# First half of the tokens first between stages, chunks split ahead behind its transposes, and the norm's diagonal on ScalarE

## The chip, the cores and the metric

The kernel runs on one core of a Trainium2 chip. A core has a matrix engine (TensorE, PE in the profile; PEld is its weight load), VectorE (DVE), ScalarE (ACT), GpSimd (POOL) and an engine that issues loads (SP). Each takes its own instructions strictly in the order in which the program gives them. The metric is the device time of one execution in microseconds (us); less is better.

## The reference, cut to what matters

256 tokens of width 1024 go through two models. The first has two layers, each a mixer and a mixture of experts; the second has two layers (l0, l1) of attention and MLP, whose norms are scaled and shifted by a projection of a condition vector.

```python
def first_block(x, ...):
    h = x
    for i in range(DEPTH):                       # 2
        mix = gla_mixer(h, ...) if i % 2 == 0 else mlstm_mixer(h, ...)
        h = layer_norm(ALPHA * h + mix, ln_g[i, 0], ln_b[i, 0])
        ffn = grouped_moe(h, router_w, moe_w1[i], moe_w3[i], moe_w2[i])
        h = layer_norm(ALPHA * h + ffn, ln_g[i, 1], ln_b[i, 1])
    return h

def rms(x, g):
    return x * lax.rsqrt(jnp.mean(x * x, axis=-1, keepdims=True) + EPS) * g

def second_block(x, c, w_ada, b_ada, ...):
    for l in range(DEPTH):                       # 2
        ada = silu(c) @ w_ada[l] + b_ada[l]
        sh1, sc1, gt1, sh2, sc2, gt2 = jnp.split(ada, 6)
        h = rms(x, g_mix[l]) * (1.0 + sc1) + sh1
        parts = jnp.split(h @ w_in[l], IN_SPLITS)
        ...                                      # two attentions, gated sum
        x = x + gt1 * (mixed @ w_out[l])
        h2 = rms(x, g_mlp[l]) * (1.0 + sc2) + sh2
        x = x + gt2 * (jnp.square(jax.nn.relu(h2 @ w_ff1[l])) @ w_ff2[l])
```

## The kernel before, in words

**Stages.** The stages run one after another: gla, moe0, mlstm, moe1, then l0 and l1. The state `h` stays on chip as two halves of 128 tokens (128 partitions x 1024); the code calls a half `mt`. A dense product needs its input turned (width on the partitions) and in two parts that sum to it, `X_H` and `X_L`, and its weights likewise as `hi` and `lo`. Three products make one: hi with X_H, lo with X_H, hi with X_L.

**Weight chunks.** Weights arrive by SP's loads into a ring of buffers `w`, 512 x 512 each, and are split in halves called chunks. `S.split` makes a chunk: ScalarE (or VectorE, by a modelled clock) casts `hi<-w`, then VectorE subtracts, `lo<-w,hi`. A dense stage calls `S.ahead(1 + LOOK)` and `S.chunk()` for each chunk, LOOK being 2: asking for its first chunk, it issues the splits of the first three, unless they were made before, and with each later chunk one more. `S.early(n)` is `S.ahead(n)` with the subtraction on GpSimd in place of VectorE. There are four buffers for hi and four for lo.

**Between stages.** Five times a stage ends in a residual and a norm whose result the next stage multiplies: moe0 to mlstm, moe1 to l0, l0's out projection to its MLP, l0 to l1, and l1's out projection to its MLP. The residual is VectorE's `res<-mm,gt` (or `res<-acc,gt`) and `h<-h,res`, by blocks of 512 columns. `rms_T` then does one half `mt`: ScalarE's squares `aff_q,ss<-h` (issued with the residual), VectorE's `rs<-ss` and `rs<-rs`, GpSimd's power `rs<-rs,mhalf`, a diagonal matrix `diag<-ident,rs` of the 128 factors. `affine_T` goes on: 16 rows of TensorE multiply the half's eight blocks of 128 x 128 with that diagonal, which turns and scales them (`tpd<-diag,h`); ScalarE makes X_H in eight pieces, `X_H<-tpd,mod`; VectorE makes eight pieces `aff_t<-tpd,mod` and two subtractions `X_L<-aff_t,X_H`. `mod` holds the scale and shift of the norm. At moe0 to mlstm a layer norm is done instead, with plain transposes and no diagonal (`ln_mv`, `ln_rs`, `ln_nb`).

**Order around it.** `out_proj` (TensorE's matmuls of the attention's last projection) and the MLP's `down(last)` take the first half's matmuls, then the second half's; at the end of each half `emit` issues the residual and the squares and pushes `rms_T` as a generator onto a list. A generator goes on by one step with each `B.tick()`, which stands behind groups of matmuls; where it yields a number it stays away for so many ticks. So the number `wait` of `affine_T` says how many groups of matmuls TensorE gets ahead of the diagonal products; where the stage has none left, the next stage's first request for the half's X (`x.wait(mt)`) ticks on until it is there. At the end of a `moe` a string sets the order in which the two halves' tails take their steps, with 'e' for an early split. The next stage's first product (`dense`) multiplies its first four chunks with the first half of the tokens and then with the second half.

**The ada stream.** The condition's projections (`w_ada`) are computed beside the other work by a generator, `ada_cols`, in quarter steps: ScalarE `ada_t<-ada_w,ccol`, VectorE a multiply-add `ada_t<-ada_w,ccol,ada_t` and an addition; after each fourth a transpose and a reduction to `part`, and TensorE folds it (`bgp<-part,fold`) into the columns of `mod`. Layer l0 has 48 quarter steps. A quarter step is issued only when a modelled clock of the engines (`calm`) finds its engine free, and at most ten ticks later. `ada_need(l, 9)`, in the first half's `emit` of `out_proj`, issues what is missing of the first 40, on which the MLP's `mod` rests.

All operations are recorded through one helper, so that the profile gives nearly all of them line 175; tiles tell them apart.

Of the kernel before, what the change touches and what calls it, by code (L numbers as in the profile page):

```python
# [30 lines left out]
AF = mybir.ActivationFunctionType  # L31
OP = mybir.AluOpType
# [195 lines left out]
def tile_model(ctx: ExitStack, tc: tile.TileContext, I, out, stages=None, h_in=None):  # L228
# [421 lines left out]
    def out_proj(x, between, emit, busy=lambda: False, each=False):  # L650


        B.hold = True
        if busy():
            B.hold = False
        ps = [[mm_ps() for _ in range(2)] for _ in range(2)]
        for nb in range(2):
            dense(x, None, KT=4, ps=ps[nb], last=False)
        between()
        chs = []  # L660
        for mt in range(2):
            for c in range(4):
                if mt == 0:
                    S.ahead(min(1 + LOOK, 4 - c))
                    chs.append(S.chunk())
                nb, c2 = divmod(c, 2)
                for k in range(2):
                    group_mm(ps[nb][mt], x, 4 + 2 * c2 + k, mt, chs[c], k, False, c2 == 1 and k == 1)
                    if k or each:
                        B.tick()  # L670
                if hooks and busy():
                    hooks.pop(0)(bg_ps())
                if mt == 1 and c in (1, 2):
                    S.early(c)
                if c2 == 1:
                    emit(mt, nb, ps[nb][mt])
        B.hold = False
# [16 lines left out]
    def affine_T(x, src, mt, gcol_, bcol_, diag=None, wait=0):  # L694


        if wait:
            yield wait
        pss = []
        for q in range(2):  # L700
            blk = lambda k: src[:, (4 * q + k) * P:(4 * q + k + 1) * P]
            if diag is None:
                ps = transpose4(blk)
            else:
                ps = mm_ps((P, 4, P), name="tpd")
                for k in range(4):
                    PE.matmul(ps[:, k], blk(k), diag, start=True, stop=True)
            pss.append(ps)
        yield
        ts = []  # L710
        for q in range(2):

            t = aff.tile([P, 4, P], F32, name="aff_t", bufs=2)
            for k in range(4):
                ka, kt = 4 * q + k, 4 * (1 - q) + k
                V.tensor_scalar(t[:, k], pss[1 - q][:, k], gcol_[:, kt:kt + 1], bcol_[:, kt:kt + 1], op0=OP.mult, op1=OP.add)
                A.activation(x.dst(0, ka, ka + 1, mt)[:, 0], pss[q][:, k], AF.Identity, scale=gcol_[:, ka:ka + 1],
                             bias=bcol_[:, ka:ka + 1])
            ts.append(t)
        for q in range(2):  # L720
            hi, lo = x.dst(0, 4 * q, 4 * q + 4, mt), x.dst(1, 4 * q, 4 * q + 4, mt)
            V.tensor_tensor(lo, ts[1 - q], hi.bitcast(F32), op=OP.subtract)
        x.ready.add(mt)
# [416 lines left out]
    def moe(l, R, tail, order, prep):  # L1140
# [344 lines left out]
        S.spare = 0  # L1485
        combine(7, y)
        tails = [tail(mt, acc[mt]) for mt in range(2)]
        n = 0
        for i in order:
            if i == 'e':  # L1490
                n += 1
                S.early(n)
            else:
                next(tails[int(i)])
        for t in tails:
            B.push(t, True)

# [484 lines left out]
    def rms_T(x, l, which, mt, wait=0, ss=None):  # L1982


        if ss is None:
            ss = small.tile([P, 2], F32, name="ss")
            for nb in range(2):
                square(ss, mt, nb)
            yield
        rs = small.tile([P, 1], F32, name="rs")  # L1990
        V.tensor_tensor(rs, ss[:, 0:1], ss[:, 1:2], op=OP.add)
        rstd(rs, rs, 1e-6, 1.0 / D)
        yield
        diag = aff.tile([P, P], F32, name="diag", bufs=2)
        V.tensor_scalar(diag, c_ident, rs, None, op0=OP.mult)
        yield from affine_T(x, h[:, mt], mt, mod[:, l, which, 0], mod[:, l, which, 1], diag, wait)

    def rms_in(l, which):
# [17 lines left out]
    def attention(l, x, at):  # L2016
# [284 lines left out]
        def emit(mt, nb, ps):  # L2301
            n = slice(nb * 512, (nb + 1) * 512)
            t = at.tile([P, 512], F32, name="res", tag="xs", bufs=4)
            V.tensor_tensor(t, ps, gt[:, n], op=OP.mult)
            V.tensor_tensor(h[:, mt, n], h[:, mt, n], t, op=OP.add)
            if nb == 0:
                sss.append(small.tile([P, 2], F32, name="ss"))
            square(sss[mt], mt, nb)
            if nb:
                if mt == 0:  # L2310
                    ada_need(l, 9)
                B.push(rms_T(x2, l, 1, mt, 1 + 3 * mt, sss[mt]), True)
        sss = []
        out_proj(mT, B.drain_urgent, emit, lambda: (l, 9) not in ada_done)
        B.hold = True
# [2 lines left out]
    def mlp(l, x, mp):  # L2318
# [29 lines left out]
        def down(fb, f, last=False, emit=None):  # L2348
            chs = []
            if not last:  # L2350
                for kt in range(4):
                    S.ahead(1 + LOOK)
                    ch = S.chunk()
                    for mt in range(2):
                        for nb in range(2):
                            n = slice(nb * 512, (nb + 1) * 512)
                            mm3(acc[mt][nb], f.get(0, kt, mt), f.get(1, kt, mt), ch[0][:, n], ch[1][:, n],
                                fb == 0 and kt == 0, False)
                    B.tick()
                    B.tick()  # L2360
                return
            for mt in range(2):
                for kt in range(4):
                    if mt == 0:
                        S.ahead(min(1 + LOOK, 4 - kt))
                        chs.append(S.chunk())
                    ch = chs[kt]
                    for nb in range(2):
                        n = slice(nb * 512, (nb + 1) * 512)
                        mm3(acc[mt][nb], f.get(0, kt, mt), f.get(1, kt, mt), ch[0][:, n], ch[1][:, n],  # L2370
                            False, kt == 3)
                    B.tick()
                    if mt == 1 and kt in (1, 2) and S.chunk_at < len(S.chunks):
                        S.early(kt)
                emit(mt)

        fx = []
# [16 lines left out]
        def emit(mt):  # L2394
# [9 lines left out]
            if nxt is None:  # L2404
                store(mt)
            else:
                B.push(rms_T(nxt, 1, 0, mt, 1 + 3 * mt, sss[mt]), True)
        sss = []
        down(7, fx[-1], True, emit)
        return nxt  # L2410
# [165 lines left out]
    if first:  # L2576
        with tc.tile_pool(name="ring_b", bufs=RB) as rb, tc.tile_pool(name="rt", bufs=1) as rp, \
# [12 lines left out]
            for i, s in enumerate(first):  # L2590
                nxt = (first + second)[i + 1] if i + 1 < len(first + second) else None
                with tc.tile_pool(name="ph_" + s, bufs=1) as ph:
# [8 lines left out]
                    else:  # L2601
# [9 lines left out]
                        B.hold = True  # L2611
                        if nxt == "mlstm":
                            xin = mlstm_in()
                            moe(l, R, lambda mt, ps: mlstm_tail(xin, mt, ps), '0e1e01', lambda: None)
                        else:
                            xin = rms_in(0, 0) if nxt == "l0" else None
                            moe(l, R, lambda mt, ps: plain_tail(mt, ps, rows, xin),
                                '0e1e00000111' if nxt else '010101',
                                lambda: rows.extend(plain_rows(l, ph)))
                if nxt is None:  # L2620
                    for mt in range(2):
# [43 lines left out]
```

## Time and profile before

| what | value |
| --- | --- |
| median of 3 runs | 1690.78 us (1687.51 to 1692.52) |
| the profiled execution, whose trace is read below | 1689.23 us |
| its span in the trace, 22598 instructions | 1687.3 us |
| mean granted TensorE clock in it | 0.969 of full speed |
| TensorE busy | 1556.7 us (92%) |
| VectorE busy | 977.3 us (58%) |
| ScalarE busy | 687.9 us (41%) |
| GpSimd busy | 224.7 us (13%) |

The profiled execution's time is its span with 1.9 us around it. Busy shares are means over stages of quite different kinds; a stage with TensorE at its full rate and a window between stages read differently, so the trace is read by windows.

### The profile page before, as it was taken

Reading aid. Unit: us, or ns where it says so; the run is one execution under the profiler, and the core shown is the slowest. Engines: PE = TensorE matmul, PEld = TensorE weight load, DVE = VectorE, ACT = ScalarE, POOL = GpSimd, SP = SyncE. Lnnn points to the kernel's source line nnn. Section 1 sums busy time; section 2 is a strip of 40 time slices with the busy share of each in tenths; the row PEclk is TensorE's granted clock in tenths of the full one; section 3 lists DMA queues with packets and bytes.
Section 4 is the critical chain, followed back from the end, with each engine's and each line's share of the span. In section 5 each row is a group of like instructions: output and inputs, shape, how many; then the busy total and the mean of one; then the engine's idle time right before and its main releaser. Section 6 shows DMA issues by size and latency. Waiting matters only on the chain.

```text
span 1687.3 us, 22598 instructions
## 1 busy us (share of the span) xinstructions
PE 1556.7 (92%) x8773; PEld 1119.2 (66%) x8774; DVE 977.3 (58%) x1644; ACT 687.9 (41%) x1118; POOL 224.7 (13%) x195
## 2 busy tenths in 40 slices
PE   7998999898999989998979999699998999999996
PEld 5865434335886644443357898499986779979995
DVE  4877113016788541111188868677778976875543
ACT  5233111113644221111146554566565555465552
POOL 1242000001243210000053100100015310020000
PEclk9999999998999989998989999899999999999999
DMA  9737899999856388999854566588875546646551
GB/s 321 292 122 269 339 372 411 406 393 195 284 194 223 121 322 347 410 402 393 318 176 161 164 186 230 159 278 296 269 262 179 168 150 176 228 172 220 179 175 50
DMA packets 165772, 422.44 MB, mean 250 GB/s; under 512 B 13018, under 2 KB 14194, under 8 KB 154643
## 3 DMA queue, kind: packets, MB, share of 16 engines
q1 hardware_dynamic: 165458, 420.75, 71.4%
q8 instruction: 73, 1.20, 0.3%
q14 instruction: 49, 0.39, 0.1%
q0 software_dynamic: 192, 0.10, 0.0%
HBM read 419.77 MB, written 1.05 MB: 249 GB/s over the span
## 4 chain that ended last, share of the span: by engine, by line
PE 27%; DVE 12%; ACT 4%; issue 3%; DMA 3%; POOL 1%; ACTq 0%; DVEq 0%; POOLq 0%
PE mm L175 17%; PE acc L175 6%; DVE lo L175 3%; DMA ada_w<-in_w_ada 3%; DVE ada_t L175 2%; ACT hi L175 1%; PE sb L175 1%; ACT pa L175 1%; DVE xs L175 1%; DVE h L175 1%; DVE th L175 1%; DVE aff_t L175 1%; DVE rt L175 1%; DVE X_L L175 0%; DVE hss L175 0%
## 5 line engine op out<-in xcount | busy, mean ns | idle before, releaser
L175 DVE TENSOR_TENSOR lo<-w,hi 128x1024 fp32r<-128x1024 f32 x274 | 342.3, 1258 | 114.3 <-ACT hi L175 113.4
L175 ACT CAST hi<-w 128x1024 fp32r<-128x1024 f32 x289 | 298.2, 1050 | 106.4 <-PE mm L175 64.0
L175 PE MATMUL mm<-hi,X_H 128*128 128x512 f32 x512 | 216.3, 423 | 16.0 <-ACT X_H L175 8.5
L175 PE MATMUL mm<-lo,X_H 128*128 128x512 f32 x512 | 207.4, 405 | 4.2 <-DVE lo L175 3.8
L175 PE MATMUL mm<-X_H,hi 128*128 128x256 f32 x704 | 202.8, 288 | 0.0
L175 PE MATMUL mm<-X_L,hi 128*128 128x256 f32 x704 | 199.1, 283 | 0.0
L175 PE MATMUL mm<-X_H,lo 128*128 128x256 f32 x704 | 199.1, 283 | 0.0
L175 PE MATMUL mm<-hi,X_L 128*128 128x512 f32 x512 | 192.8, 400 | 3.6 <-DVE X_L L175 3.5
L175 PE MATMUL up<-w,X 128*64 128x512 f32 x672 | 193.4, 596 | 0.8 <-ACT X L175 0.8
L175 PEld LDWEIGHTS mm<-X_H,hi 128*128 128x128 f32 x704 | 134.5, 191 | 1.7 <-issue 0.7
L175 PEld LDWEIGHTS mm<-X_L,hi 128*128 128x128 f32 x704 | 134.6, 191 | 0.4
L175 PEld LDWEIGHTS mm<-X_H,lo 128*128 128x128 f32 x704 | 134.6, 191 | 0.0
L175 PEld LDWEIGHTS mm<-hi,X_H 128*128 128x128 f32 x512 | 99.8, 195 | 48.0 <-issue 13.3
L175 PEld LDWEIGHTS up<-w,X 128*64 128x64 f32 x672 | 58.5, 137 | 96.5 <-issue 92.4
L175 DVE SCALAR_TENSOR_TENSOR y<-dn,gsl,y 128x512 fp32r<-128x512 f32 x32 | 24.0, 751 | 161.6 <-ACT y L175 161.6
L175 PEld LDWEIGHTS mm<-lo,X_H 128*128 128x128 f32 x512 | 99.9, 195 | 26.4 <-DVE lo L175 7.8
L175 PEld LDWEIGHTS mm<-hi,X_L 128*128 128x128 f32 x512 | 97.8, 193 | 29.1 <-DVE X_L L175 7.6
L175 PE MATMUL up<-wh,X 128*64 128x512 f32 x336 | 116.1, 603 | 0.0
L175 PE MATMUL dn<-w,hTt 128*64 128x512 f32 x336 | 105.1, 629 | 2.1 <-ACT hTt L175 2.1
L175 PE MATMUL acc<-lo,fh 128*128 128x512 f32 x256 | 100.7, 393 | 0.3 <-DVE lo L175 0.3
L175 PE MATMUL acc<-hi,fl 128*128 128x512 f32 x256 | 100.8, 394 | 0.0
L175 PE MATMUL acc<-hi,fh 128*128 128x512 f32 x256 | 99.6, 389 | 0.0
(412 smaller groups left out, 2577.0 us busy)
## 6 DMA issues: line engine op xcount, KB each, us to landing
w<-in_moe_w SPq DMA_DIRECT2D x126, 1024.0 KB, 9.7
w<-in_w_ff SPq DMA_DIRECT2D x64, 1024.0 KB, 5.5
wh<-in_moe_w SPq DMA_DIRECT2D x124, 512.0 KB, 11.5
ada_w<-in_w_ada SPq DMA_DIRECT2D x96, 512.0 KB, 5.3
w<-in_w_in SPq DMA_DIRECT2D x40, 1024.0 KB, 5.2
w<-in_mlstm_w_in SPq DMA_DIRECT2D x16, 1024.0 KB, 19.1
w<-in_gla_w_in SPq DMA_DIRECT2D x12, 1024.0 KB, 9.6
w<-in_w_out SPq DMA_DIRECT2D x8, 1024.0 KB, 5.1
```

Source lines behind the costliest of these rows:

```text
L175: r = f(*args, **kw)
```

## The change

Four edits, all of them to what is issued between stages, and in which order.

- Early splits leave the last matmuls of `out_proj` and of the MLP's `down`, and the order strings of `moe`. In their place `affine_T` calls `S.early(1)` for the first half, right behind its transposes: one chunk, where there were two.
- At three places inside l0 and l1 the first half's wait was 1 tick and becomes -1, which `affine_T` now takes as a yield of 0: the generator goes on at its very next tick, one sooner than before. The second half's stays 4.
- The order strings bring the first half's tail forward: at moe1 to l0 its steps come first.
- The diagonal `diag<-ident,rs` is made by ScalarE (`activation` with Copy and a scale), no more by VectorE.

```diff
@@ out_proj
                 if hooks and busy():
                     hooks.pop(0)(bg_ps())
-                if mt == 1 and c in (1, 2):
-                    S.early(c)
                 if c2 == 1:
                     emit(mt, nb, ps[nb][mt])
@@ affine_T
         if wait:
-            yield wait
+            yield max(wait, 0)
         pss = []
...
             pss.append(ps)
+        if mt == 0:
+            S.early(1)
         yield
@@ moe
         tails = [tail(mt, acc[mt]) for mt in range(2)]
-        n = 0
         for i in order:
-            if i == 'e':
-                n += 1
-                S.early(n)
-            else:
-                next(tails[int(i)])
+            next(tails[int(i)])
@@ rms_T
         diag = aff.tile([P, P], F32, name="diag", bufs=2)
-        V.tensor_scalar(diag, c_ident, rs, None, op0=OP.mult)
+        A.activation(diag, c_ident, AF.Copy, scale=rs)
@@ layer2, emit of out_proj (the same edit in mlp, emit)
-                B.push(rms_T(x2, l, 1, mt, 1 + 3 * mt, sss[mt]), True)
+                B.push(rms_T(x2, l, 1, mt, 5 * mt - 1, sss[mt]), True)
@@ mlp, down
                     B.tick()
-                    if mt == 1 and kt in (1, 2) and S.chunk_at < len(S.chunks):
-                        S.early(kt)
                 emit(mt)
@@ the orders at the end of moe0 and of moe1
-                            moe(l, R, lambda mt, ps: mlstm_tail(xin, mt, ps), '0e1e01', lambda: None)
+                            moe(l, R, lambda mt, ps: mlstm_tail(xin, mt, ps), '0101', lambda: None)
...
-                                '0e1e00000111' if nxt else '010101',
+                                '00001010' if nxt else '010101',
```

What the diff doesn't tell is how the instructions stand on each engine. On ScalarE, where l0's MLP ends and l1 begins (`aff_q,ss<-h` is a half's square, `hi<-w` a chunk's cast, `X_H<-tpd,mod` a half's X_H; a sign at the front says before or after):

```order
 L175 ACTIVATE ada_t<-ada_w,ccol 128x512 x2
 L175 ACTIVATE aff_q,ss<-h 128x512 x2
-L175 CAST hi<-w 128x1024 x2
+L175 ACTIVATE diag<-ident,rs 128x128
+L175 CAST hi<-w 128x1024
+L175 ACTIVATE X_H<-tpd,mod 128x128 x8
 L175 ACTIVATE aff_q,ss<-h 128x512 x2
-L175 ACTIVATE X_H<-tpd,mod 128x128 x8
-L175 CAST hi<-w 128x1024 x2
+L175 CAST hi<-w 128x1024 x2
+L175 ACTIVATE diag<-ident,rs 128x128
+L175 CAST hi<-w 128x1024
```

Before, both early casts stand between the first half's squares and the second's, and the next two casts behind X_H of the first half; now one cast stands behind the first diagonal, X_H of the first half ahead of the second half's squares, and the casts of the second to the fourth chunk behind them, the fourth behind the second diagonal.

On VectorE at the same place, from the first half's step in `rs` on (`lo<-w,hi` is a chunk's subtraction, `aff_t` and `X_L` make the turned half's lower part, `res` and `h` are the second half's residual):

```order
-L175 TENSOR_SCALAR diag<-ident,rs 128x128
+L175 TENSOR_SCALAR aff_t<-tpd,mod 128x128 x8
+L175 TENSOR_TENSOR X_L<-aff_t,X_H 128x512 x2
 L175 TENSOR_TENSOR res<-acc,gt 128x512
 L175 TENSOR_TENSOR h<-h,res 128x512
 L175 TENSOR_TENSOR res<-acc,gt 128x512
 L175 TENSOR_TENSOR h<-h,res 128x512
-L175 TENSOR_SCALAR aff_t<-tpd,mod 128x128 x8
-L175 TENSOR_TENSOR X_L<-aff_t,X_H 128x512 x2
+L175 TENSOR_TENSOR lo<-w,hi 128x1024 x2
 L175 TENSOR_TENSOR rs<-ss 128x1
 L175 TENSOR_SCALAR rs<-rs 128x1
```

The first diagonal is gone, the first half's eight `aff_t` and two `X_L` now stand ahead of the second half's residual, and two chunk subtractions stand between that residual and the second half's `rs`; one stood behind it before.

On VectorE at the end of l0's out projection, from the first half's first residual on (`ada_t<-ada_w,ccol,ada_t` is the ada stream's multiply-add of one quarter step, `ada_t<-ada_t` its addition, `raw<-bgp` the copy behind its fold):

```order
 L175 TENSOR_TENSOR res<-mm,gt 128x512
 L175 TENSOR_TENSOR h<-h,res 128x512
-L175 STREAM_TRANSPOSE ada_t<-ada_t 128x512
-L175 TENSOR_REDUCE part<-ada_t 128x16
+L175 SCALAR_TENSOR_TENSOR ada_t<-ada_w,ccol,ada_t 128x512
+L175 TENSOR_TENSOR ada_t<-ada_t 128x512
 L175 TENSOR_TENSOR res<-mm,gt 128x512
 L175 TENSOR_TENSOR h<-h,res 128x512
-L175 COPY raw<-bgp 128x4
+L175 SCALAR_TENSOR_TENSOR ada_t<-ada_w,ccol,ada_t 128x512
+L175 TENSOR_TENSOR ada_t<-ada_t 128x512
+L175 STREAM_TRANSPOSE ada_t<-ada_t 128x512
```

Two quarter steps of the stream that stood ahead of this residual before, in the attention, now stand behind it: 34 of l0's are issued ahead of it, where 36 were.

## Rows read from the trace of the kernel before

The columns of a timeline are: start in the span, duration (both us), engine, line, operation, output and inputs, shape, count, and in brackets the idle time before it and what ended it.

**Rows 1.** The page: busy time of each engine, and its two costliest groups.

```profile
PE 1556.7 (92%) x8773; PEld 1119.2 (66%) x8774; DVE 977.3 (58%) x1644; ACT 687.9 (41%) x1118; POOL 224.7 (13%) x195
...
L175 DVE TENSOR_TENSOR lo<-w,hi 128x1024 fp32r<-128x1024 f32 x274 | 342.3, 1258 | 114.3 <-ACT hi L175 113.4
L175 ACT CAST hi<-w 128x1024 fp32r<-128x1024 f32 x289 | 298.2, 1050 | 106.4 <-PE mm L175 64.0
```

**Rows 2.** Windows: stretch, length, PE, PEld, DVE, ACT, POOL busy, clock, DMA, GB/s.

```profile
1264.00:1289.00 25.00, 19.06 (x89) 14.66 (x88) 21.76 (x39) 13.09 (x29) 13.43 (x17) 0.93 0.55 189
880.00:1040.00 160.00, 153.09 (x1073) 132.07 (x1072) 129.90 (x255) 89.87 (x177) 26.82 (x26) 0.99 0.59 185
```

**Rows 3.** Timeline of TensorE where l0 goes over to l1.

```profile
1271.48 2.02 PE L175 MATMUL tpd<-diag,h 128*128 128x128 f32 x16 [2.13 <-DVE diag L175]
...
1276.65 0.58 PE L175 MATMUL mm<-hi,X_H 128*128 128x512 f32 x1 [3.15 <-ACT X_H L175]
...
1282.85 2.02 PE L175 MATMUL tpd<-diag,h 128*128 128x128 f32 x16
```

**Rows 4.** Timeline of VectorE at the same place.

```profile
1264.33 0.68 DVE L175 TENSOR_TENSOR res<-acc,gt 128x512 f32<-128x512 f32 x1
...
1268.93 2.40 DVE L175 TENSOR_SCALAR diag<-ident,rs 128x128 f32<-128x128 f32 x1 [0.73 <-POOL rs L175]
...
1271.96 2.15 DVE L175 TENSOR_TENSOR h<-h,res 128x512 f32<-128x512 f32 x1
...
1280.48 0.15 DVE L175 TENSOR_SCALAR rs<-rs 128x1 f32<-128x1 f32 x1
```

**Rows 5.** Timeline of VectorE, second half, l1's out projection to its MLP.

```profile
1492.84 0.29 DVE L175 TENSOR_SCALAR diag<-ident,rs 128x128 f32<-128x128 f32 x1 [0.45 <-POOL rs L175]
...
1497.95 1.30 DVE L175 TENSOR_TENSOR X_L<-aff_t,X_H 128x512 fp32r<-128x512 f32 x2
```

**Rows 6.** Timeline of GpSimd where l0 goes over to l1.

```profile
1268.35 0.55 POOL L175 TENSOR_TENSOR rs<-rs,mhalf 128x1 f32<-128x1 f32 x1 [15.05 <-DVE rs L175]
1268.90 4.67 POOL L175 TENSOR_TENSOR lo<-w,hi 128x1024 fp32r<-128x1024 f32 x2
```

**Rows 7.** Timeline of ScalarE at the same place.

```profile
1267.10 0.63 ACT L175 ACTIVATE aff_q<-h 128x512 f32<-128x512 f32 x1 [0.60 <-DVE h L175]
...
1276.16 2.89 ACT L175 ACTIVATE X_H<-tpd,mod 128x128 fp32r<-128x128 f32 x8
```

**Rows 8.** Timeline of TensorE, both halves, l1's out projection to its MLP.

```profile
1482.61 2.05 PE L175 MATMUL tpd<-diag,h 128*128 128x128 f32 x16 [1.07 <-DVE diag L175]
...
1493.24 1.99 PE L175 MATMUL tpd<-diag,h 128*128 128x128 f32 x16
```

**Rows 9.** Timeline of TensorE, l0's out projection to its MLP.

```profile
1068.16 0.29 PE L175 MATMUL bgp<-part,fold 128*32 128x4 f32 x8 [12.56 <-DVE part L175]
...
1075.71 1.95 PE L175 MATMUL tpd<-diag,h 128*128 128x128 f32 x16
...
1085.11 1.98 PE L175 MATMUL tpd<-diag,h 128*128 128x128 f32 x16
```

**Rows 10.** Timeline of VectorE, moe1 to l0.

```profile
848.21 1.43 DVE L175 TENSOR_TENSOR rs<-ss 128x1 f32<-128x1 f32 x1 [0.79 <-ACT aff_q L175]
```

**Rows 11.** Timeline of TensorE, moe1 to l0.

```profile
850.92 3.75 PE L175 MATMUL tpd<-diag,h 128*128 128x128 f32 x16 [8.00 <-DVE diag L175]
...
862.35 1.95 PE L175 MATMUL tpd<-diag,h 128*128 128x128 f32 x16
```

**Rows 12.** Timeline of VectorE, moe0 to mlstm.

```profile
398.82 1.65 DVE L175 SCALAR_TENSOR_TENSOR ln_nb<-ln_mv,ln_rs 128x1 f32<-128x1 f32 x1
```

**Rows 13.** Timeline of ScalarE, the ada stream ahead of l0's MLP.

```profile
1057.28 1.32 ACT L175 ACTIVATE ada_t<-ada_w,ccol 128x512 f32<-128x512 f32 x2
...
1062.72 0.72 ACT L175 ACTIVATE ada_t<-ada_w,ccol 128x512 f32<-128x512 f32 x1 [4.12 <-DMA ada_w<-in_w_ada]
```

**Rows 14.** Windows: the diagonal products where moe1 goes over to l0.

```profile
851.00:854.50 3.50, 3.50 (x16) 3.37 (x16) 2.41 (x4) 1.66 (x6) 0.00 (x0) 0.50 0.96 339
```

More of the change, by code (lines that the diff above doesn't have):

```diff
@@ L2406, in emit @@
             else:
-                B.push(rms_T(nxt, 1, 0, mt, 1 + 3 * mt, sss[mt]), True)
+                B.push(rms_T(nxt, 1, 0, mt, 5 * mt - 1, sss[mt]), True)
         sss = []
```

## Prediction

> **What bounds the kernel now.** I read the page's busy times first: TensorE is busy 92% of the span, VectorE 58% [rows 1]. Inside a stage there is little to win: over the 160 us of l0's attention TensorE is busy 153 [rows 2]. The windows between stages are another matter: 19.1 of 25 us at the step from l0 to l1 [rows 2]. The change is worth what it does at five places, which I number B1 (moe0 to mlstm, about 400 us), B2 (moe1 to l0, 850), B3 (l0's out projection to its MLP, 1070), B4 (l0 to l1, 1270) and B5 (l1's out projection to its MLP, 1480). The next stage's first four weight chunks are c0 to c3; (0) and (1) are the two halves of the tokens.
>
> Then I took each engine's timeline at B4. TensorE waits 2.13 us for the diagonal, runs its 16 rows of diagonal products, and waits 3.15 us for ScalarE's X_H [rows 3]. VectorE shows why: the diagonal takes 2.40 us and an addition into h 2.15 us [rows 4], where such a diagonal takes 0.29 [rows 5] and the neighbouring products 0.68 [rows 4]; both end when one of GpSimd's two subtractions for c0 and c1 ends, which together last from 1268.90 to 1273.57 [rows 6]. After that TensorE has c0 and c1 ready and goes straight to the second half's diagonal products at 1282.85 [rows 3]. The reader should see both sides: the early subtractions hold VectorE up, and they are what lets TensorE run once X_H is there.
>
> **The blocked VectorE.** B4's rows give back 2.1 + 1.5 us if GpSimd stays out of the way. The Trainium skill, SBUF — State Buffer, "Who interferes with whom", says that a VectorE instruction with two SBUF inputs, or in a two-port mode, waits for a GpSimd instruction that reads SBUF, to its end. The trace agrees (2.40 against 0.29 [rows 4, 5]); by that rule alone the change should gain wherever the early split stood, and its time is the first rival's.
>
> **The change part by part.**
>
> *What goes.* One of two early chunks: c1 is no longer cast and subtracted ahead; nor does c0's subtraction stand before the diagonal. c1's cast now comes with c2's, when the next stage asks for its first chunk, which is behind everything the second half has issued by then.
>
> *What is gained before X_H(0).* At B4 the diagonal is free when the power ends at 1268.90 [rows 6]. On ScalarE it is an operation the trace does not show; the nearest rows are X_H's 128x128 pieces, 2.89 for eight, 0.36 each [rows 7], and the 512 wide square, 0.63 [rows 7]. I take 0.4, being the same shape as the pieces; the two diagonals of a place cost or give 0.2 us by the bounds. With 0.15 to TensorE the products start at 1269.45, 2.0 earlier than 1271.48. At B5 the second half's sum for the ada rows now meets the power, so I take 1.4 (bounds 1.0 to 2.0) from 1482.61 [rows 8]. At B3 nothing was blocked there; the products move ahead of the last six of 24 matmuls that filled the 7.55 us up to them [rows 9], worth 1.3.
>
> *What is added behind it.* From the start of the diagonal products to the end of X_L(0) I take the undisturbed second half at B5: 1493.24 to 1497.95 + 1.30 [rows 5, 8], 6.0 us. In the new order VectorE only then does the residual product and addition of the second half (0.68 each: 1.35 at B3 and B5, where one block is left; 2.7 at B4, where both are) [rows 4]. ScalarE's square waits for it (0.65 to its successor) [rows 7], and c1's cast waits for the square (1.05) [rows 1]. Then VectorE: c1's and c2's subtractions (2 x 1.2; the page's mean is 1.26 with overlap) [rows 1], the two rs steps (0.35; one is 0.15) [rows 4]; GpSimd's power 0.7 with its hand-over (0.55) [rows 6]; the second diagonal 0.4; c3's cast, which stands behind it on ScalarE, 1.05; c3's subtraction 1.2; and TensorE takes two matmuls of c3 (0.3) before the second diagonal products. The sum is 6.0 + 1.35 + 0.65 + 1.05 + 2.4 + 0.35 + 0.7 + 0.4 + 1.05 + 1.2 + 0.3 = 15.4 us from first to second products at B3 and B5, and 16.8 at B4. Before, it was 9.4 at B3 [rows 9], 11.4 at B4 [rows 3] and 10.6 at B5 [rows 8]. Subtracting the earlier start, the second products come later by 15.4 - 9.4 - 1.3 = **4.7** (B3), 16.8 - 11.4 - 2.0 = **3.4** (B4), 15.4 - 10.6 - 1.4 = **3.4** (B5). What hangs on them (X_H(1), X_L(1), the second half's matmuls) keeps its distance: X_L(1) is ready 5.4 after the products' start [rows 5, 8], and TensorE's own work up to there was as long. So TensorE trades 5 us of waits for a longer one: c0's four matmuls, then nothing until c1.
>
> *B2.* VectorE's rs sum is no longer held (1.43 against 0.15) [rows 10], and the products start 1.5 earlier than 850.92 [rows 11], at 849.4 (bounds 1.0 to 2.0). They run 3.75 there [rows 11], so X_L(0) ends 3.75 + 4.0 later, at 857.2. Now the second half's two multiplications (1.4), three subtractions (3.6), the rs steps (0.35) and, since the second products now stand behind all of the first half's matmuls, eight of these (0.23 each, 1.8): 864.4 instead of 862.35 [rows 11], **+2.0**.
>
> *B1.* There is no diagonal. The 128x1 bias step, 1.65 because GpSimd is in its subtraction [rows 12], becomes one of 0.15, so the transposes start 1.5 sooner; c1's subtraction is again late, but TensorE fills part of it with the second half's transposes. **-1.4** (bounds -3 to +1).
>
> *The ada stream.* Its steps are placed where a modelled clock finds room, and less is found: before out projection's first residual in l0 34 quarter steps have been issued instead of 36 of the 40 that the MLP's modulation needs. At that point TensorE already waits 12.56 us for the stream [rows 9]. There a pair of quarters takes 1057.28 to 1062.72, 5.4 us, 4.12 of it waiting for a load [rows 13]. Two more quarters cost 1.4 (a quarter's VectorE steps alone) to 5.4; the first now loads beside the residual, so I take **+4.0**. In return attention has two quarters less on VectorE, some 4 us of work in a stage where TensorE lost 6.9 us in all [rows 2]: **-1.5** (0 to -4).
>
> *The clock.* After 8.00 us of waiting the diagonal's 16 rows took 3.75, after 2.13 they took 2.02 [rows 3, 11]; the granted clock was 0.50 there, the lower of its two levels, 1.2 GHz [rows 14]. A wait of some 6 us at B4 lies between. Most matmuls it would slow stand before c3's subtraction, which they wait for anyway: **+0.5** (0 to 3). The Trainium skill, TensorE: Matmul & The Clock Gate, Part 1, says an idle array falls to half its clock; that speaks against a change that turns short waits into one long one, and by it the term would be nearer 2.
>
> *Loads.* The weight buffer that c1 frees is free 5 to 8 us later and its next load is issued so much later on SP's queue; that load serves c8, more than 70 matmuls (16 us) on: nothing.
>
> *The sum:* -1.4 + 2.0 + 4.7 + 3.4 + 3.4 + 4.0 - 1.5 + 0.5 = **+15 us**. The profiled execution took 1689.23 us (span 1687.3), 1.6 below the median of the three timed runs; 1689.2 + 15.1 = **1704 us**. With the bounds the likeliest case runs from 1696 to 1713.
>
> **The rivals.** *First, the blocked time comes back whole (faster).* What VectorE lost to GpSimd's subtractions is gained and nothing takes its place: 2.1 + 1.5 at B4, 2.1 at B5, where TensorE waits for the diagonal too [rows 8], 1.3 at B2 and 1.5 at B1, 8.5 in all: 1689.2 - 8.5 = 1681. The rule of the Trainium skill's SBUF — State Buffer weighed above would have it so. It decides if c1's subtraction ends before X_L(0) does. For it: the blocked rows. Against it: the order puts c1's cast behind the second half's square on ScalarE. *Second, the two sides cancel (same).* The ada stream's two quarters are found room for in the earlier attention, and at B3 to B5 the chain is shorter than its sum by 2 us each because ScalarE and VectorE run the rs steps beside the subtractions: 15 - 4 - 6 = 5 or less, about 1693. Against it: each engine takes its instructions in order, and the rs steps stand behind c2's subtraction. *Third, the stream's stall is worse (slower still):* both quarters wait a load in full, 8.2 instead of 4.0, and the lower clock costs its 3: 1704 + 4 + 3 = 1711.
>
> **Chances.** The forecast 0.66, the third rival 0.06, the second 0.16, the first 0.12. A measurement tells about 0.3% here (5 us). Faster by more than that: 0.12; within it: 0.16; slower: 0.72. The range leaves out the first rival and what lies above 1712: 1689 to 1712.
>
> **What would show it.** Right: at B4 and B5 VectorE without a step over 2 us, ScalarE's X_H(0) some 4 us earlier, then a wait of TensorE of 4 to 6 us for c1's subtraction, the second products near 15 us after the first, and over 15 us of waiting for the ada stream at B3. Wrong: TensorE running through from c0 to c3, or the second products within 11 us of the first; then the chain overlaps where I added it up, and the time is nearer the first or second rival.

## The result and the profile after

The changed kernel takes 1707.4 us (median of 4 runs, 1704.11 to 1710.15) against 1690.84 (4 runs, 1687.51 to 1692.52): the ratio is 1.0100, with a 95% interval of 1.0079 to 1.012, so it is slower by 16.6 us, by the interval 13 to 20. The forecast was 1704, range 1689 to 1712.

The page of the profiled execution (1706.79 us), its span and its busy times:

```profile
span 1704.9 us, 22589 instructions
PE 1559.2 (91%) x8774; PEld 1123.0 (66%) x8774; DVE 968.8 (57%) x1642; ACT 691.4 (41%) x1126; POOL 212.1 (12%) x189
```

The work is the same as in [rows 1]; what grew is waiting. TensorE's timeline at B4 (start, us, engine, line, operation, tiles, shape, idle time before and its releaser):

```profile
1280.28 2.05 PE L175 MATMUL tpd<-diag,h 128*128 128x128 f32 x16 [1.10 <-ACT diag L175]
...
1284.25 0.39 PE L175 MATMUL mm<-lo,X_H 128*128 128x512 f32 x1
1290.74 0.80 PE L175 MATMUL mm<-hi,X_H 128*128 128x512 f32 x1 [6.10 <-ACT hi L175]
1292.00 0.80 PE L175 MATMUL mm<-lo,X_H 128*128 128x512 f32 x1 [0.46 <-DVE lo L175]
...
1296.79 0.50 PE L175 MATMUL mm<-lo,X_H 128*128 128x512 f32 x1 [0.39 <-DVE lo L175]
1297.13 1.95 PE L175 MATMUL tpd<-diag,h 128*128 128x128 f32 x16
```

This answers to [rows 3]. The wait of 3.15 us for X_H is gone, and one of 6.10 for c1's cast stands in its place; the second products start 16.85 us after the first, where it was 11.37. VectorE at the same place, which answers to [rows 4]:

```profile
1285.05 1.29 DVE L175 TENSOR_TENSOR X_L<-aff_t,X_H 128x512 fp32r<-128x512 f32 x2
1286.26 0.68 DVE L175 TENSOR_TENSOR res<-acc,gt 128x512 f32<-128x512 f32 x1
1286.98 0.69 DVE L175 TENSOR_TENSOR h<-h,res 128x512 f32<-128x512 f32 x1
...
1290.72 2.36 DVE L175 TENSOR_TENSOR lo<-w,hi 128x1024 fp32r<-128x1024 f32 x2 [1.72 <-ACT hi L175]
1293.00 0.15 DVE L175 TENSOR_TENSOR rs<-ss 128x1 f32<-128x1 f32 x1
```

No single step takes over 2 us any more (the 2.36 us are two subtractions). The second residual stands behind X_L, two subtractions behind that, and only then the second `rs`. ScalarE (against [rows 7]):

```profile
1279.83 0.40 ACT L175 ACTIVATE diag<-ident,rs 128x128 f32<-128x128 f32 x1 [1.04 <-POOL rs L175]
1280.14 1.03 ACT L175 CAST hi<-w 128x1024 fp32r<-128x1024 f32 x1
1281.48 1.50 ACT L175 ACTIVATE X_H<-tpd,mod 128x128 fp32r<-128x128 f32 x4 [0.32 <-PE tpd L175]
...
1289.66 1.97 ACT L175 CAST hi<-w 128x1024 fp32r<-128x1024 f32 x2
1294.00 0.40 ACT L175 ACTIVATE diag<-ident,rs 128x128 f32<-128x128 f32 x1 [2.36 <-POOL rs L175]
```

The diagonal takes 0.40 us there, and c1's and c2's casts start 9.5 us after c0's, behind the second squares. The chain of work that ended last here, from GpSimd's power for the second `rs` on (start, us, what):

```profile
1293.42 0.55 POOL rs L175
1293.97 0.02 issue
1294.00 0.40 ACT diag L175
1294.40 0.95 ACT hi L175
1295.35 0.02 issue
1295.37 1.38 DVE lo L175
1296.75 0.04 issue
1296.79 0.50 PE mm L175
1297.29 1.80 PE tpd L175 x16
```

At B4 it runs as the prediction's sum does: power, diagonal, c3's cast behind it, c3's subtraction, matmul, products.

**Where the time went.** The same matmul stands in both traces; the difference of its starts, after less before, grows at a few places only. For instance the second fold ahead of l0's MLP started at 1068.16 [rows 9] and now at 1075.06, 6.90 later:

```profile
1062.99 0.29 PE L175 MATMUL bgp<-part,fold 128*32 128x4 f32 x8 [6.57 <-DVE part L175]
1075.06 0.29 PE L175 MATMUL bgp<-part,fold 128*32 128x4 f32 x8 [11.78 <-DVE part L175]
```

The table has, for the changed kernel and each experiment, what the lag grew by at each place (median over the matmuls of a stretch behind it, less that ahead of it), all against the one trace of before. Ahead of 840 us two executions differ by up to 5 us, whatever the edit, and e4, e7, e8 and e11, which are alike up to l0, by 0.5 at B2, so single entries under 1 say little; the changed kernel and e3, which are the same from l0's MLP on, agree within 0.4 there. The ratio is to runs of the kernel before made beside each experiment (medians 1688.6 to 1690.8 us), so it does not follow from the time alone.

| run | B2 | l0 attention | ada stall | B3 | B4 | B5 | time | ratio to before, 95% |
| --- | --- | --- | --- | --- | --- | --- | --- | --- |
| after | +3.2 | +0.7 | +4.9 | +5.5 | +2.5 | +3.4 | 1707.4 | 1.0100 (1.0079 to 1.012) |
| e1 order only | 0.0 | -0.2 | -0.4 | +5.9 | +6.0 | +6.1 | 1709.0 | 1.0127 (1.0104 to 1.015) |
| e2 c1 behind X_L | +2.7 | +1.1 | +4.8 | +7.0 | +4.1 | +4.9 | 1717.0 | 1.0178 (1.0141 to 1.0215) |
| e3 old moe1 order | +1.5 | +0.2 | -0.3 | +5.8 | +2.8 | +3.4 | 1698.6 | 1.0062 (1.0037 to 1.0086) |
| e4 ScalarE diagonal only | +0.6 | +0.2 | -0.1 | +0.1 | -2.0 | -1.0 | 1687.1 | 0.9981 (0.9967 to 0.9995) |
| e5 old orders | +1.6 | +0.2 | -0.4 | +5.9 | +0.5 | +0.4 | 1698.7 | 1.0056 (1.0035 to 1.0077) |
| e6 TensorE kept busy | +3.3 | +0.9 | +5.1 | +5.0 | +1.6 | +3.4 | 1866.7 | 1.1065 (1.1035 to 1.1095) |
| e7 ada stream sooner | +0.1 | +8.4 | -13.3 | -0.1 | +0.2 | -1.0 | 1685.5 | 0.9979 (0.9963 to 0.9995) |
| e8 second rs first | +0.6 | +0.2 | -0.4 | +1.8 | -3.0 | -1.1 | 1687.4 | 0.9995 (0.9978 to 1.0012) |
| e9 two early chunks | +0.7 | +1.2 | +4.8 | +6.7 | +4.2 | +6.0 | 1711.3 | 1.0130 (1.0100 to 1.0161) |
| e10 VectorE diagonal | +5.8 | +1.9 | +4.8 | +5.2 | +5.0 | +4.1 | 1717.9 | 1.0189 (1.0154 to 1.0223) |
| e11 ada a little sooner | +0.6 | +7.9 | -7.9 | -0.3 | +0.2 | +0.3 | 1688.1 | 0.9984 (0.9965 to 1.0002) |

For the changed kernel these sum to 20.2. With -1.8 up to moe1's end, -1.0 inside l0's MLP (most runs show it, with the change's edits or without, so it is this trace of before) and +0.3 in l1's attention that is 17.7; the two profiled executions differ by 17.6.

### The profile page after: what moved, and what is told of

Read it like the earlier page. It is cut to its first block, busy times and chain, and to the rows that moved or that the text cites. A ratio compares the mean times of both kernels' runs of the same rounds, so it can differ in the third digit from the quotient of the medians.

```text
span 1704.9 us, 22589 instructions
## 1 busy us (share of the span) xinstructions
PE 1559.2 (91%) x8774; PEld 1123.0 (66%) x8774; DVE 968.8 (57%) x1642; ACT 691.4 (41%) x1126; POOL 212.1 (12%) x189
## 4 chain that ended last, share of the span: by engine, by line
PE 34%; DVE 8%; ACT 3%; issue 3%; DMA 1%; POOL 1%; DVEq 0%; POOLq 0%; ACTq 0%
PE mm L175 21%; PE acc L175 9%; DVE lo L175 2%; DMA ada_w<-in_w_ada 1%; PE sb L175 1%; DVE aff_t L175 1%; ACT hi L175 1%; ACT pa L175 1%; DVE xs L175 1%; PE tpd L175 1%; DVE ada_t L175 1%; DVE X_L L175 1%; POOL hss L175 1%; PE adar L175 0%; DVE h L175 0%
## 5 line engine op out<-in xcount | busy, mean ns | idle before, releaser
L175 DVE TENSOR_TENSOR lo<-w,hi 128x1024 fp32r<-128x1024 f32 x278 | 347.9, 1261 | 135.8 <-ACT hi L175 131.3
L175 PE MATMUL mm<-hi,X_H 128*128 128x512 f32 x512 | 218.5, 427 | 24.7 <-ACT hi L175 16.5
```

The source lines that it names most:

```text
L175: r = f(*args, **kw)
```

## The experiments

**Theory A**: the row of work that VectorE, ScalarE and GpSimd do one after the other from the first half's X_L to the second half's diagonal sets the places B3 to B5, and the new order lengthens it. **Theory B**: TensorE misses the second early chunk, c1.

**e1, the order alone**, in the kernel before.

```diff
-            yield wait
+            yield max(wait, 0)
...
-                B.push(rms_T(x2, l, 1, mt, 1 + 3 * mt, sss[mt]), True)
+                B.push(rms_T(x2, l, 1, mt, 5 * mt - 1, sss[mt]), True)
```

> The kernel before with one edit: the first half's wait of 1 tick becomes -1 at the three places in l0 and l1, so that its diagonal products and its X go ahead of the second half's residual; both early chunks stay where they were and VectorE makes the diagonal. Theory A (the order is what costs: the second half's residual, square, casts and subtractions stand in a row behind X_L of the first half): first to second diagonal products 13 us where one residual block is left (B3, B5) and 14.4 at B4, against 9.4, 10.6 and 11.4 before; time 1696 to 1700. Theory B (the missing second early chunk is what costs): the order alone is harmless, distances within 1 us of before, time 1687 to 1691.

1709.0 us, 6 at each of the three places: B falls, and A was too small (1696 to 1700). TensorE at B4:

```profile
1278.38 3.14 PE L175 MATMUL tpd<-diag,h 128*128 128x128 f32 x16 [3.50 <-DVE diag L175]
...
1289.93 0.79 PE L175 MATMUL mm<-hi,X_H 128*128 128x512 f32 x1 [3.75 <-ACT hi L175]
...
1294.44 3.62 PE L175 MATMUL tpd<-diag,h 128*128 128x128 f32 x16
```

The wait of 3.75 us is for c2's cast, with c0 and c1 long there. The distance from first to second products is 16.06 us (expected 14.4; at B3 and B5 15, expected 13), and the products themselves take 3.14 and 3.62 instead of 2.0, so the lower clock falls on work that the rest waits for.

**e2, c1 split sooner**, in the changed kernel.

```diff
             V.tensor_tensor(lo, ts[1 - q], hi.bitcast(F32), op=OP.subtract)
+        if mt == 0:
+            S.ahead(2)
         x.ready.add(mt)
```

> The changed kernel with one edit: the second chunk c1 is cast right behind the first half's X_H and subtracted on VectorE right behind the first half's X_L, ahead of the second half's residual. TensorE has c1 some 3 us after X_L instead of after 5 to 7. Theory A (VectorE's and ScalarE's row of work up to the second diagonal sets the time): the subtraction only changes its place in the row, the second products come at the same time within 0.7 us at B3 to B5, TensorE's wait is cut in two; time 1704 to 1708. Theory B (TensorE misses c1): 3 to 4 us are won at each of B3, B4, B5; time 1695 to 1699.

B fails again, and the time is above both ranges, 9.6 us worse than the changed kernel. Of that, 4.6 us stand at B3 to B5; 5.2 stood already ahead of 840 us (+3.4 where the changed kernel has -1.8) and are not explained by the edit. The distance from first to second products at B4 is 17.10 us, about as in the changed kernel (16.85), as A says. What A had not in it: TensorE's one long wait became six shorter ones, and the lower clock moved onto the second products. The windows over these products in e2 and in the changed kernel (stretch, length, PE, PEld, DVE, ACT, POOL busy, clock, DMA, GB/s):

```profile
1304.17:1307.56 3.39, 3.39 (x18) 3.39 (x17) 0.70 (x2) 1.44 (x4) 3.39 (x7) 0.56 0.82 266
```

```profile
1297.13:1299.08 1.95, 1.95 (x18) 1.95 (x17) 0.97 (x2) 0.86 (x3) 1.95 (x4) 1.00 0.54 121
```

In the changed kernel TensorE runs from 1292 on with hardly a pause and has the full clock (1.00, 2.4 GHz) again before the products; in e2 it waits 0.94 and 0.60 us in the last 3 us ahead of them, and they run at 0.56, mostly the lower level.

**e3, the old order at moe1**, in the changed kernel: `'0100000111'` for `'00001010'`.

> The changed kernel with the old order of the tails at the end of moe1 (without its early splits). By the order in which they are issued, 36 quarter steps of the ada stream then stand ahead of l0's first residual again instead of 34. If the displaced quarters are what cost in the stream's stall, TensorE's waits for the fold ahead of l0's MLP fall from 18.3 us in two to 13 to 14, and the time falls by 4 to 5 us and by what the step from moe1 to l0 gives besides (0 to 2): 1701 to 1704. If the stall is from something else (the loads' pace, or the later start of l0), it stays at 17 to 19 us and the time at 1706 to 1708.

The stall went: the fold's waits are 0.99 and 12.22 us, as before. So the 4.9 us come from the two displaced quarters, and it is the order of moe1's tails that displaced them. The time, 1698.6 us, is 2.4 below the range's lower end; B2 gave 1.7 besides.

**e4, the diagonal alone**, in the kernel before.

```diff
-        V.tensor_scalar(diag, c_ident, rs, None, op0=OP.mult)
+        A.activation(diag, c_ident, AF.Copy, scale=rs)
```

> The kernel before with one edit: ScalarE makes the diagonal. By the order it then stands ahead of the early casts, so that GpSimd's subtractions start about 1.5 us later too. If what VectorE lost to GpSimd is won and kept: at B4 the first products start 1.5 to 2 us earlier, VectorE's residual of the second half is done ahead of the subtractions, X_H comes 3 to 4 us earlier, and B2 and B5 give 1 to 2 each; time 1681 to 1686. If the wait only moves (the early chunks come later, or the blocked steps are others): 1688 to 1692.

Between the two: 2 to 3 us are won. VectorE at B4 in e4:

```profile
1266.57 0.69 DVE L175 TENSOR_TENSOR h<-h,res 128x512 f32<-128x512 f32 x1
1267.18 0.69 DVE L175 TENSOR_TENSOR res<-acc,gt 128x512 f32<-128x512 f32 x1
1267.90 2.46 DVE L175 TENSOR_TENSOR h<-h,res 128x512 f32<-128x512 f32 x1
1270.28 1.36 DVE L175 TENSOR_SCALAR aff_t<-tpd,mod 128x128 f32<-128x128 f32 x4
```

GpSimd's two subtractions run from 1267.44 to 1272.57. They block another step, the second addition into h, and TensorE still waits 3.0 us for X_H. The four `aff_t`, whose input is in PSUM, take their usual 1.36 us with GpSimd at work.

**e5, the old orders**, in the changed kernel: e3's edit and the waits of before.

> The changed kernel with the old waits (1 and 4) and the old order of the tails at moe1: of the change there remain the diagonal on ScalarE, the early chunk behind the first half's transposes (one instead of two), and moe0's order. Run e1 put the cost on the order. If that holds, the three places B3 to B5, which cost 5.5, 2.5 and 3.4 us in the changed kernel, cost between -1 and +1.5 each here, the ada stream's stall is that of before, and the time is 1686 to 1692. If the missing second early chunk costs by itself, TensorE waits 3 us or more for c1 at each of them, and the time is 1694 or more.

Right at B4 and B5 (+0.5 and +0.4), wrong at B3 (+5.9), and the time of 1698.7 us is in the other reading's range, though TensorE does not wait 3 us for c1 at each place. VectorE at B3:

```profile
1078.64 0.69 DVE L175 TENSOR_TENSOR res<-mm,gt 128x512 f32<-128x512 f32 x1 [0.73 <-PE mm L175]
1079.37 2.67 DVE L175 TENSOR_TENSOR h<-h,res 128x512 f32<-128x512 f32 x1
```

With the early chunk behind the transposes GpSimd's subtraction of c0 falls on the residual that now stands there. Against e4, which is e5 with both early chunks at their old places, the new place costs 5.8, 2.5 and 1.4 us at B3 to B5; here TensorE does wait for c1 (2.3 us at B3). So B holds a part where A's order is undone. The edits do not add up: order alone 6 at B3, early place alone 6, both together 5.5.

**e6, TensorE kept busy**, in the changed kernel.

```diff
                     chs.append(S.chunk())
+                if mt == 0 and c == 1:
+                    for _ in range(16):
+                        PE.matmul(ps[mt], x.get(0, k0, mt), chs[0][0][:, 0:512], start=False, stop=False)
```

> The changed kernel with 16 more matmuls of 512 columns (c0 with X_H again, added into the same sum, so that what the stages compute is another thing) between the matmuls of c0 and of c1 in a stage's first product, in the wait of 3.8 to 6.1 us for c1; some 3.7 us of work. TensorE's clock then has less reason to fall. If the lower clock behind that wait is a small cost, because c3's subtraction comes later than the slow matmuls end, the second products at B3 to B5 come 0 to 0.8 us sooner each. If the clock is what makes the wait dear, they come 1.5 to 2 us sooner each, for matmuls of 0.40 instead of 0.63 us. Where TensorE does not wait so long (the places ahead of l0) the extra work costs up to 3.7 us each; time 1703 to 1713, which says little, and the places are what is read.

Its time says nothing: what is computed is another thing, and moe1 alone takes 154 us longer. The places can be read: 0.5, 0.9 and 0.0 us won at B3 to B5. The 0.9 at B4 lies ahead of the first products, for which TensorE waits 0.23 us instead of 1.10; from first to second products e6 is 0.35, 0.00 and 0.02 us shorter. TensorE at B3:

```profile
1243.76 4.46 PE L175 MATMUL mm<-hi,X_H 128*128 128x512 f32 x17
1248.98 0.50 PE L175 MATMUL mm<-lo,X_H 128*128 128x512 f32 x1 [0.76 <-DVE lo L175]
1249.32 0.40 PE L175 MATMUL mm<-hi,X_H 128*128 128x512 f32 x1
...
1253.64 0.50 PE L175 MATMUL mm<-lo,X_H 128*128 128x512 f32 x1 [0.75 <-DVE lo L175]
1253.98 1.95 PE L175 MATMUL tpd<-diag,h 128*128 128x128 f32 x16
```

At B3 and B5 the matmuls behind the wait take 0.40 instead of 0.63 us, and then TensorE waits for c3's subtraction (0.75 us at B3): nearly all that the lower clock had cost there would have been waited anyway. At B4, where a wait of 2.46 us is left, part of them stay slow.

**e7 and e11, the ada stream sooner**: e4, and in l0 a limit of 1 tick (e7) or 2 (e11) instead of 10 in `calm`.

> The kernel before with the diagonal on ScalarE (run e4) and, in l0 alone, a limit of one tick instead of ten on how long each step of the ada stream waits for a free moment. All 42 quarter steps then stand ahead of l0's first residual by the order. If the stall ahead of l0's MLP is a matter of how many quarter steps are issued by then, the 13 us of waits for the fold vanish and the attention pays 3 to 8 us on VectorE for the steps that it takes up: 1676 to 1683. If the loads set the stream's pace, TensorE waits as long inside the attention: 1685 to 1690.

> Run e7 with a limit of two ticks instead of one in l0: 38 quarter steps ahead of l0's first residual instead of 42 (36 in the kernel before). Run e7 won 13.3 us of stall and lost 8.4 in the attention. If a quarter that goes through in the attention costs less than its share of the stall, this lies between: the attention pays 2 to 4 us, the stall falls by 5 to 7, 1684 to 1687 all told. If the stall hangs on the loads, it falls by less than 2 us: 1687 to 1690.

e7's stall vanishes, as the first reading has it, but the attention pays 8.4 of the 13.3 us, a little over the 3 to 8 allowed for, and the time is in the second reading's range. Its window over the attention, to set beside [rows 2]:

```profile
880.00:1040.00 160.00, 150.18 (x1041) 129.09 (x1040) 127.73 (x252) 90.76 (x179) 27.27 (x27) 0.97 0.58 185
```

TensorE gets 1041 matmuls done there where it did 1073. e7 is the fastest median here, 1685.5 us, but its interval overlaps that of e4 wholly. e11 falsifies both of its readings: two quarters fewer through the attention, the same price there (7.9), and only 7.9 of the stall won.

**e8, the second `rs` right behind its residual**, in e4.

```diff
-                B.push(rms_T(x2, l, 1, mt, 1 + 3 * mt, sss[mt]), True)
+                g = rms_T(x2, l, 1, mt, (1, 3)[mt], sss[mt])
+                if mt:
+                    next(g)
+                B.push(g, True)
```

> The kernel before with the diagonal on ScalarE (run e4), and the second half's rs steps issued right behind its residual instead of behind the first half's X_L, with a wait of 3 ticks instead of 4 for its transposes (the three places inside l0 and l1). By the order the second diagonal products then stand ahead of the first half's last four matmuls with X_L and need no chunk but c0 and c1. If the row of work from the second residual to the second diagonal is what sets these places, the second products come 2 to 3 us sooner at each; time 1677 to 1682. If they then wait as long for ScalarE (which makes X_H of the first half ahead of the diagonal) or GpSimd, 1685 to 1690.

The distances fall as A says, though by 1.7 us each and not by 2 to 3, from 8.85, 11.12 and 10.71 us in e4 to 7.20, 9.43 and 9.03. The time does not: at B3 the second products take 3.60 us at a clock of 0.53, mostly the lower level, and behind B4 2.9 us are lost again by the end of l1's attention.

**e9, both early chunks behind the transposes**, in the changed kernel: `S.early(2)` for `S.early(1)`.

> The changed kernel with both early chunks behind the first half's transposes instead of one (cast by ScalarE ahead of X_H, subtracted by GpSimd, one after the other, some 4.7 us). VectorE then has one subtraction less (1.2 us) between the second residual and the second rs, but X_H of the first half comes a cast (1.0 us) later, and X_L may wait for GpSimd's end. If the row of work up to the second diagonal sets the time, the places B3 to B5 stay within 1 us each of the changed kernel's 5.5, 2.5 and 3.4: 1704 to 1710. If TensorE's missing c1 sets it, 2 to 3 us are won at each: 1698 to 1701.

c1 is there in time, and B3 to B5 get worse, 6.7, 4.2 and 6.0, by more than the 1 us that A allowed; distances are 16.5 to 16.7, and the second products take 2.9 to 3.6 us, which with the distances makes up the difference. Only B2 wins (2.5). The time is 1.3 us over A's range. B is out at B3 to B5, and holds at B2.

**e10, the diagonal back on VectorE**, in the changed kernel.

> The changed kernel with the diagonal back on VectorE. On ScalarE the cast of c0 then stands right behind the first half's squares, so that GpSimd may start c0's subtraction as soon as its power is done, at the moment when VectorE would make the diagonal. If that blocks the diagonal as in the kernel before (2.4 us instead of 0.3), the first products come 2 us later at B4 and B5 and the time is 1709 to 1713, and the ScalarE edit is worth that much in the changed kernel. If the diagonal is through before the subtraction starts, nothing changes: 1705 to 1709.

1717.9 us, 5 above the range's end. VectorE and GpSimd at B4:

```profile
1284.01 2.38 DVE L175 TENSOR_SCALAR diag<-ident,rs 128x128 f32<-128x128 f32 x1 [0.73 <-POOL rs L175]
```

```profile
1283.96 2.34 POOL L175 TENSOR_TENSOR lo<-w,hi 128x1024 fp32r<-128x1024 f32 x1
```

GpSimd starts 0.05 us ahead of VectorE, and the diagonal waits for its end; these places cost 2.6 us more at B2, 2.5 at B4 and 0.7 at B5. Here moving the diagonal is what keeps the early chunk from blocking it. The 1.2 us more in l0's attention and the rest of the difference to 1717.9 are not explained.

## Why the prediction was right

The time came out 3 us above the forecast. No term was off by more than 2.2 us, and most were too small.

**What is gained ahead of X_H(0)**: right. Taking off the lag ahead of each place, the first products are earlier by 1.8 (B2), 1.0 (B3), 2.6 (B4) and 1.7 us (B5); forecast were 1.5, 1.3, 2.0 and 1.4. ScalarE's diagonal takes 0.40, as taken. X_H(0) comes 6.1 us earlier at B4 and 3.7 at B5, where the sign was some 4.

**The row behind it**: right in size, and in its mechanism at B4. From first to second products the sum gave 15.4, 16.8 and 15.4 us at B3 to B5; the trace has 15.86, 16.85 and 15.73. The costs of 4.7, 3.4 and 3.4 measured 5.5, 2.5 and 3.4. The wait for c1 was forecast as 4 to 6 us and is 3.8 at B3 and B5, 6.1 at B4, but it is no price by itself: e2 and e9 give TensorE c1 sooner, and the distance stays at 15.8 to 17.1 us, since VectorE's and ScalarE's row is as long. What the sum did not have is a second path that ends as late. At B3, and at B5 likewise, c3's subtraction is done before TensorE comes to it (VectorE, then TensorE):

```profile
1095.56 1.23 DVE L175 TENSOR_TENSOR lo<-w,hi 128x1024 fp32r<-128x1024 f32 x1 [2.04 <-ACT hi L175]
```

```profile
1090.91 0.80 PE L175 MATMUL mm<-hi,X_H 128*128 128x512 f32 x1 [3.79 <-ACT hi L175]
1092.17 0.79 PE L175 MATMUL mm<-lo,X_H 128*128 128x512 f32 x1 [0.47 <-DVE lo L175]
...
1096.61 0.59 PE L175 MATMUL mm<-lo,X_H 128*128 128x512 f32 x1
...
1097.51 1.95 PE L175 MATMUL tpd<-diag,h 128*128 128x128 f32 x16
```

From c1's subtraction on TensorE runs 13 matmuls there without a wait, most of them at the lower clock, straight into the second products. In e6, where they run at the full clock and TensorE does wait for c3, the distance is 0.35 us shorter at B3 and 0.02 at B5. So row and matmuls end within 0.4 us of each other, and that the sum of the one gave the time of both is in part luck.

**B1 and B2**: B1 measured -1.3 against -1.4, but the runs with B1's old order (e1, e4, e7, e8, e11) have between +0.3 and -1.0 there, so a gain is hardly shown. B2's +2.0 was 1.2 too small. Its first products take 3.78 us, as taken; what the sum lacked is c1:

```profile
854.99 0.80 PE L175 MATMUL mm<-hi,X_H 128*128 128x512 f32 x1 [2.83 <-ACT hi L175]
857.58 0.79 PE L175 MATMUL mm<-lo,X_H 128*128 128x512 f32 x1 [1.79 <-DVE lo L175]
...
863.84 1.95 PE L175 MATMUL tpd<-diag,h 128*128 128x128 f32 x16
```

From 857.58 on TensorE runs all that is left of the first half's matmuls without a pause up to the second products; the second diagonal was ready at 861.01. Here it is c1 that sets the time, and e9, with c1 made early, wins 2.5 us.

**The ada stream**: +4.0 was 4.9, and e3 shows the cause. **-1.5 for the attention** was wrong in sign (+0.7): VectorE's busy time from 880 to 1040 us fell from 129.9 [rows 2] to 127.4, and TensorE's did not rise (152.1 for 153.1):

```profile
880.00:1040.00 160.00, 152.10 (x1070) 131.72 (x1069) 127.40 (x253) 89.11 (x176) 25.16 (x22) 0.99 0.56 178
```

Fewer steps on an engine that is not the bound won nothing: the five runs with the order that leaves 34 quarter steps have +0.7 to +1.9 us in the attention, those with 36 have -0.2 to +0.2. In e7 six quarter steps more do cost; why two fewer don't pay is open.

**The clock**: +0.5 was about right for the changed kernel at B3 to B5 (e6: 0.4 us between first and second products, over three places). The reason given, that the slowed matmuls wait for c3's subtraction anyway, is what the rows show at B4; at B3 and B5 they don't wait, and the term is small because the row ends as late. It would have been wrong for other orders, as e1, e2, e8 and e9 show.

**The rivals.** The first, that blocked time comes back whole, had its gain (the earlier first products) but not its condition: at B4 the matmul that waits for c1's subtraction starts at 1292.00, 5.7 us after X_L(0) ends (1285.05 + 1.29). Its 2.1 at B5 was VectorE's loss; TensorE's wait there is 1.07 [rows 8]. The rule of the Trainium skill, SBUF — State Buffer, "Who interferes with whom", on which it leaned holds in these traces, also where the change and the experiments moved the conflict (2.46, 2.67 and 2.38 us in e4, e5 and e10). The same section says that a VectorE instruction with at most one SBUF input, outside its two-port modes, does not contend with GpSimd; the `aff_t` of e4, 1.36 us beside GpSimd's subtraction, agree. The prediction told the rule for VectorE alone; in the trace of before it goes the other way too: at B5 VectorE's subtraction starts at 1491.16, GpSimd's power at 1491.31, and the power takes 1.49 us instead of 0.55 [rows 6]. The second rival needed chains shorter by 2 us each; they were longer by 0.5 at B3. The third needed a stall of 8.2 us; it was 4.9.

## What to carry to other kernels

A wait that is named for one instruction is not yet a price: ask what the next meeting point needs, here the second diagonal, and sum each engine's row up to it in issue order, TensorE's own matmuls too. An edit that leaves the longest row as long wins nothing (e2 and e9 at B3 to B5), and one that shortens it need not pay either (e8). Before reordering, look at what a time-modelled planner places by that order elsewhere: a changed string at moe1 cost 5 us 200 us later. And of two edits that each put work ahead of the same meeting point, measure them together, since neither their costs nor their gains add up.

## What the runs showed of the hardware

What a wait of TensorE costs by the lower clock is not told by the wait: it depends on which matmuls then run slowly, and on whether anything waits for them. In the changed kernel at B4, waits of 6.10 and 0.46 us for c1 were followed by five us with hardly a pause, the first matmuls of these were slow, and the second products ran at 1.95 us (clock 1.00). In e1, e2 and e9 shorter waits came between c1 and the second products, the last ones just ahead of them, and the same 16 rows took 2.9 to 3.6 us at all three places (clock 0.56 in e2 at B4). The sum of the waits does not order these cases: in the 11 us ahead of the second products at B4 it is 6.9 us in the changed kernel and 4.8 in e1. Nor does their number: in e5 at B5 four waits of 0.76 to 1.02 us left the products at 1.95. No rule for it is shown here. The Trainium skill, TensorE: Matmul & The Clock Gate, Part 1, says that an idle array falls to half its clock; the 0.80 us of the first matmul behind the 6.10 us, where others take 0.39, and the granted clock of 0.50 from 1290.7 to 1293 us, the lower of the two levels, agree.
